# Row statistics of the attention read at the head of a chunk, and those of the first output tiles later

## The chip, the core and the metric

The kernel runs on one core of a Trainium2 chip. Its time is device time in microseconds (us). The engines are named as in the profile: PE is TensorE (matrix products; PEld its weight loads), DVE is VectorE, ACT is ScalarE, POOL is GpSimd, SP issues most of the DMAs. Each engine takes its instructions strictly in its own order and waits at an instruction until what it needs has been signalled by the others.

## What is computed

One layer of a streaming encoder for 1024 prompt frames, 64 frames of a running stream and 16 meta tokens, width 1024. One input projection gives queries, keys, values, gates and the inputs of a convolution. One half is attention over chunks of 64 frames (own chunk, two before it, the meta tokens, a learned sink per head), the other a causal depthwise convolution of width 31 with LayerNorm, SiLU and a pointwise product. Both halves are RMS-normalised per frame, multiplied by a SiLU gate, and go through one output projection:

```python
y = concat([rms(att, g_att) * silu(ga), rms(conv, g_conv) * silu(gb)]) @ w_out
h = h + rms(y, g_post)
```

The two inner `rms` need, per frame, one over the root of a mean of squares over 512 channels. These are the row statistics of the title: `ra` for the attention half, `rc` for the convolution half.

## The kernel before, in words

The frames lie in three column groups (0 to 384, 384 to 768, 768 to 1104). Input products are units `g` of 24 matmuls each (weight tile and frames split in a high and a low part, three products): `g19_1` is weight tile 19, column group 1. A unit's result lies in one PSUM bank until its reader has taken it: for the attention gate tiles (12 to 15) and the last convolution gate tile (19) the reader is ACT (a tanh) and then DVE (`ga` or `gb`, a multiplication that is put off by some steps). Three banks with the tag `mm` serve these units, the `ra` and the `var` alike (`mm_ps`, line 125). A bank is given to the next tile that asks for one when its last reader so far is known; the bank whose reader was recorded first goes first.

The units wait in a queue. The attention loop (lines 959 to 1007) goes through the 17 chunks in the order 16 (the running stream), 0, 1, ... 15, and puts `fill(n)`, that is n matmuls of the queue, between its own steps, so that PE has work while the other engines do theirs. In turn i it records: the score products `s` of chunk order[i] with four DVE passes that read them (`att_scores`, line 651), gate multiplications, the products `av` with the values for chunk order[i-2] (`att_values`, 719), the split `qs` of the next queries (`att_prep`, 646), the transposes `pa` and `pb` for chunk order[i-1] (`att_transpose`, 703), the exponentials, the normalisation `T` (`norm`, 679), and, at the end of the turn, `att_stats` for chunk order[i-3]. From turn L0 on (that of chunk 11) LayerNorm steps stand among them, for three column groups n: `ln_pre` sums four channel tiles on DVE, `ln_mean` is a product `mu`, a subtraction on DVE, squares on ACT (`vq`) and their sums on POOL, `ln_var` is three tiny products `var` and their DVE reads `rln`, `ln_diag` prepares a diagonal on DVE (`sqc`), `ln_scale` is a product `rstd` and a multiplication of `H` on DVE.

`att_values` also leaves, for each tile of two chunks, the sum of squares over channels in `asq` (ACT squares, two POOL additions). `att_stats` (740) turns it into row statistics: a product `ra` of `asq` with a column of ones into a bank `mm`, a DVE operation `ra4t` (for tile 4) that reads it, and a power on POOL.

The last stage is the pointwise product `pw` (four column groups by four tiles) with a small task of a list, `plan`, behind each of the 16: the letters l, h are the splits of the output weights, M, n the splits of an output tile's operands (ACT, DVE), and `r0`, `r1` are `rc_rstd(0)` and `rc_rstd(1)` (line 1081): a product `rc` into the one bank `av`, a DVE operation `rc0t`, a power on POOL. Then come the output tiles T = 0, 1, 8, 2, ... 7, each with products `y`; `rc_rstd(T + 1)` is called behind the last product of tile T where it hasn't been called yet, and `rc_rstd(0)` and `rc_rstd(8)` within tile 0.

The order of each engine's instructions is that in which they are recorded; only two counters, which estimate how far PE, DVE and ACT have got (`given`, line 67), decide on which of ACT and DVE a few operations go, and put off others.

Of the kernel before, what the change touches and what calls it, by code (L numbers as in the profile page):

```python
# [33 lines left out]
NCHUNK = SEQ // HD  # L34
# [14 lines left out]
def layer_kernel(ctx: ExitStack, tc: tile.TileContext, x, x_fm, w_in, w_pw, w_out, vec, g_post,  # L49
# [70 lines left out]
    def chunks(ap):  # L120
        return ap.rearrange("p (c q) -> p c q", q=HD)
# [3 lines left out]
    def mm_ps(name):  # L125
        banks[0] += 1
        run_due(lambda p: p[1] and p[1] <= banks[0] - 3)
        return ps_tile("mm", 3, name)
# [61 lines left out]
    def hi_w(p, on_dve=False, dst=None, a=0, b=KT):  # L190
        m = WORDER[p]
        load_raw(p)
        if not a:
            pre[m] = dst or (wp.tile([P, KT, P], F32R, tag="whi", name=f"whi{m}"),
                             wp.tile([P, KT, P], F32R, tag="wlo", name=f"wlo{m}"))
        raw, hi = halves[a] if p == 2 else raws[p][:, a:b], pre[m][0][:, a:b]
        if on_dve:
            dve.tensor_copy(hi, raw)
        else:
            act.activation(hi, raw, AF.Copy)  # L200

    def lo_w(p, a=0, b=KT, on_dve=False):
        hi, lo = (t[:, a:b] for t in pre[WORDER[p]])
        raw = halves[a] if p == 2 else raws[p][:, a:b]
        if p > 3 and not on_dve and freer() == "act":
            act.activation(lo, hi.bitcast(F32), AF.Copy, scale=-1.0)
            pool.dma_start(out=lo, in_=raw, accum_op=ALU.add)
            return
        dve.tensor_tensor(out=lo, in0=raw, in1=hi.bitcast(F32), op=ALU.subtract)
# [189 lines left out]
    def fill(k):  # L399
        for _ in range(min(k, len(queue))):  # L400
            queue.pop(0)()
            tick()
# [189 lines left out]
    def row_rstd(src, r, dst, name, ps):  # L592
        for o in range(0, P, r):
            mm(ps[o:o + r, 0:2], lhsT=src, rhs=ones_m[:, 0:2], start=True, stop=True)
        r = P
        t = sm.tile([P, 1], F32, tag="rr", bufs=2, name=name + "t")
        dve.tensor_scalar(out=t[:r], in0=ps[:r, 0:1], scalar1=RMS_EPS, scalar2=None,
                                op0=ALU.add)
        pool.tensor_tensor(out=dst[:r], in0=t[:r], in1=mhalf[:r], op=ALU.pow)
# [46 lines left out]
    def att_prep(c):  # L646
        qs = kqs[c] = sm.tile([P, 2, 4, HD], F32R, tag="qs", bufs=2, name=f"qs{c}")
        act.activation(qs[:, 0], qb[:, c], AF.Copy)
        dve.tensor_tensor(out=qs[:, 1], in0=qb[:, c], in1=qs[:, 0].bitcast(F32), op=ALU.subtract)
# [41 lines left out]
    def att_v(c):  # L691

        if c % 2 == 0:
            nc.sync.dma_start(vE[MB:MB + HD], vtok[:HD, c // 2])
            avs[c] = [(NKEY, vE)]
            if c:
                avs[c].insert(0, (2 * HD, vcache if c == NCHUNK else vtok[:, c // 2 - 1]))
        else:
            if c > 1:
                nc.sync.dma_start(vO[:HD], vtok[HD:, c // 2 - 1])  # L700
            avs[c] = [(HD + MB, vO if c > 1 else vE), (NKEY, vtok[:, c // 2])]

    def att_transpose(c):
        lo, T = att[c]
        pt = slot("P", f"PT{c}", (P, 2, 512))
        att[c] = []
        for n, (end, v) in enumerate(avs.pop(c)):
            k = end - lo
            ps = ps_tile("pt", 2, f"p{'ab'[n]}{c}")
            for i in range(4):  # L710
                tp(ps[:k, i * P:(i + 1) * P], T[:, i, lo:end], ident)
            if freer() == "act":
                act.activation(pt[:k, n, :], ps[:k, :], AF.Copy)
            else:
                dve.tensor_copy(pt[:k, n, :], ps[:k, :])
            att[c].append((k, v, pt[:, n]))
            lo = end

    def att_values(c):
        sample = c == NCHUNK  # L720
        av = ps_tile("av", 1, f"av{c}")
        last = len(att[c]) - 1
        for n, (k, v, pt) in enumerate(att[c]):
            for g in range(2):
                mm(av[g * HD:(g + 1) * HD, :256], lhsT=v[:k, g * HD:(g + 1) * HD],
                   rhs=pt[:k, g * 256:(g + 1) * 256], start=n == 0, stop=n == last)
        av4 = av[:, :256].rearrange("p (t q) -> p t q", t=4)
        act.activation(qb[:, c], av4, AF.Copy)
        Tt = c // 2
        if Tt not in asq:  # L730
            asq[Tt] = sm.tile([P, 4, P], F32, tag="asq", bufs=2, name=f"asq{Tt}")
        o = (c % 2) * HD
        act.activation(asq[Tt][:, :, o:o + HD], qb[:, c], AF.Square)
        if c % 2 or sample:
            w = HD if sample else P
            s = asq[Tt]
            pool.tensor_tensor(out=s[:, 0:2, :w], in0=s[:, 0:2, :w], in1=s[:, 2:4, :w], op=ALU.add)
            pool.tensor_tensor(out=s[:, 0, :w], in0=s[:, 0, :w], in1=s[:, 1, :w], op=ALU.add)

    def att_stats(Tt):  # L740
        w = HD if Tt == 8 else P
        row_rstd(asq[Tt][:, 0, :w], w, ra[:, Tt:Tt + 1], f"ra{Tt}", mm_ps(f"ra{Tt}"))
# [11 lines left out]
    h1, h2 = (0, 4), (4, KT)  # L754
# [127 lines left out]
    def gate_att(ready, most=12):  # L882
        for g in [g for g in gas if all(c in ready for c in range(g[2] // HD, g[3] // HD))][:most]:
            gas.remove(g)
            t, n, c0, c1, gt = g
            dst = qb[:, c0 // HD:c1 // HD, t, :]
            dve.tensor_tensor(out=dst, in0=dst, in1=chunks(gt[:, :c1 - c0]), op=ALU.mult)
# [64 lines left out]
    order = [NCHUNK] + list(range(NCHUNK))  # L952
# [5 lines left out]
    i = -1  # L958
    while (i := i + 1) < max(len(order) + 2, L0 + 7 if L0 < 99 else 0):
        left = len(order) + 1 - i  # L960
        if L0 == 99 and i >= 9 and (i == 12 or len(taps) < 2):
            L0 = i
        quota = (max(24, -(-(len(queue) - REST) // left)) if i else 48) if left > 0 else 26
        n = i - L0
        if i < len(order):
            exps, norm = att_scores(order[i])
        if n > 0:
            gate_att(order[:max(0, i - 2)], 2)
        if 2 < i <= len(order) + 1:
            att_values(order[i - 2])  # L970
        if 1 < i < len(order):
            att_v(order[i])
        if i == len(order) + 1:
            hi_w(len(WORDER) - 1, on_dve=True, dst=[sm.tile([P, KT, P], F32R, tag=t, bufs=1, name=f"w1{t}")
                                          for t in ("kT", "vT")])
            lo_w(len(WORDER) - 1, on_dve=True)
        if i + 1 < len(order):
            att_prep(order[i + 1])
        fill((32 if i == 1 else 4) if left > 0 else 0)
        if 0 < i <= len(order):  # L980
            att_transpose(order[i - 1])
        if i < len(order):
            exps()
        fill(8 if left > 0 else 4)
        if n == 0:
            while taps:
                f, j = taps.pop(0)
                f(j)
            sqc = sm.tile([P, HW], F32, tag="sq", bufs=1, name="sqc")
        for step, at in ((ln_pre, (0,1,3)), (ln_diag, (2, 4, 6))):  # L990
            if n in at:
                step(at.index(n))
        if i < len(order):
            norm()
        fill(8 if left > 0 else 4)
        if i == 1:
            att_values(order[0])
            att_v(order[1])
        if 3 <= i < len(order) + 3:
            c = order[i - 3]  # L1000
            if c % 2 or c == NCHUNK:
                att_stats(c // 2)
        for step, d in ((ln_mean, 0), (ln_var, 1), (ln_scale, 2)):
            if n - d in (0, 2, 4):
                fill(2)
                step((n - d) // 2)
        fill((quota - 20 if left > 0 else 8) - (2 if 0 <= n <= 6 else 0))
# [99 lines left out]
    drain()  # L1107
    run_due(lambda p: True)

    plan = "G0,l1,h2 l2,h3 l3,S2 h4 z2 l4,h5 l5,S3 h6 z3,h7 l6,M0 l7,r0 n0 . r1 M1 n1".split()  # L1110
    for n in range(4):
        for m in range(4):
            pointwise(n, m, [pre[PW], pre[PW + 1]])
# [136 lines left out]
```

## Time and profile before

| | before |
|---|---|
| time, median of 3 runs | 483.17 us (482.18 to 485.7) |
| the profiled execution | 482.85 us |
| its span (first to last instruction) | 481.1 us |
| busy: PE, DVE, ACT, POOL | 461.8, 380.0, 231.9, 75.0 us |
| mean granted clock of PE in the span | 0.986 |

The span leaves out 1.75 us of the profiled execution that lie around it. A clock of 1 stands for the higher of PE's two levels, 2.4 GHz; 0.5 is the lower, 1.2 GHz.

### The profile page before, as it was taken

What the parts mean: (1) busy time and instruction counts of PE and PEld (TensorE: products, weight loads), DVE (VectorE), ACT (ScalarE), POOL (GpSimd) and SP (SyncE); (2) the same over time, 40 slices, a digit from 0 to 9 for tenths busy, and PEclk for the clock granted to TensorE, in tenths of its full rate; (3) what the DMA queues carried; (4) which work ended last, traced back from release to release, by engine and by line L of the source; (5) the groups of instructions that cost most, each with busy time, mean ns of one, the idle gap of its engine ahead of it and who ended that gap; (6) DMA issues with size and microseconds to landing.
All of it is one profiled execution on the core that took longest, in us unless ns stands there. A gap on an engine that the chain in (4) does not pass through costs nothing.

```text
span 481.1 us, 7432 instructions
## 1 busy us (share of the span) xinstructions
PE 461.8 (96%) x2809; PEld 420.3 (87%) x2809; DVE 380.0 (79%) x671; ACT 231.9 (48%) x535; POOL 75.0 (16%) x106
## 2 busy tenths in 40 slices
PE   8999999999999999999999996989998999999994
PEld 7999999999999999988889885868898887888884
DVE  3669999999999999988999995666999545645443
ACT  6675432135133225567667755545787325433322
POOL 0000100003010000001201223232224501111100
PEclk9999999999999999999999998889999999999998
DMA  8992244044033334230110101011243212222231
GB/s 275 402 330 97 44 102 114 0 110 131 4 82 89 90 88 93 67 92 4 51 35 19 50 4 47 5 48 44 89 132 131 89 65 89 65 89 88 87 122 54
DMA packets 16491, 43.54 MB, mean 91 GB/s; under 512 B 2600, under 2 KB 4888, under 8 KB 16456
## 3 DMA queue, kind: packets, MB, share of 16 engines
q1 hardware_dynamic: 14584, 37.31, 22.9%
q0 software_dynamic: 1872, 5.77, 6.4%
q8 instruction: 22, 0.36, 0.3%
q14 instruction: 13, 0.11, 0.1%
HBM read 32.00 MB, written 4.84 MB: 77 GB/s over the span
## 4 chain that ended last, share of the span: by engine, by line
PE 75%; DVE 11%; ACT 2%; issue 1%; DMA 1%; POOL 0%; DVEq 0%; POOLq 0%; ACTq 0%
PE g L104 44%; PE y L104 20%; PE av L104 3%; PE s L104 3%; DVE H L86 2%; DVE wo L86 2%; PE pa L108 1%; DVE sqc L86 1%; PE pb L108 1%; DMA woraw<-in_w_out_dram 1%; DVE qb L86 1%; DVE T L86 1%; ACT T L86 1%; PE pw L104 1%; DVE zl L86 1%
## 5 line engine op out<-in xcount | busy, mean ns | idle before, releaser
L104 PE MATMUL g<-xT,whi 128*128 128x384 f32 (+2 forms) x960 | 225.4, 334 | 0.4 <-DVE xT L86 0.2
L104 PEld LDWEIGHTS g<-xT,whi 128*128 128x128 f32 x960 | 169.0, 189 | 8.9 <-issue 6.1
L86 DVE SCALAR_TENSOR_TENSOR H<-u,vec_t,H 128x1118 f32<-128x1118 f32 x120 | 166.5, 1388 | 3.2
L104 PE MATMUL g<-xT,wlo 128*128 128x384 f32 (+2 forms) x480 | 139.6, 333 | 0.5 <-DVE wlo L86 0.5
L104 PEld LDWEIGHTS g<-xT,wlo 128*128 128x128 f32 x480 | 88.3, 189 | 2.7 <-issue 1.2
L104 PE MATMUL y<-wo,mh 128*128 128x512 f32 (+2 forms) x304 | 89.0, 381 | 0.0
L104 PEld LDWEIGHTS y<-wo,mh 128*128 128x128 f32 (+1 forms) x304 | 55.2, 185 | 11.5
L104 PE MATMUL y<-wo,ml 128*128 128x512 f32 (+1 forms) x136 | 51.2, 378 | 0.0
L86 DVE SCALAR_TENSOR_TENSOR y<-y,small,y 128x512 f32<-128x512 f32 (+1 forms) x19 | 13.7, 721 | 32.8 <-PE y L104 29.4
L86 ACT ACTIVATE T<-T,st 128x210 f32<-128x210 f32 (+2 forms) x85 | 37.0, 450 | 5.0 <-DVE st L86 4.9
L86 POOL DMA_DIRECT2D wlo<-wraw x13 | 11.5, 885 | 148.8 <-ACT wlo L86 123.7
L104 PEld LDWEIGHTS y<-wo,ml 128*128 128x128 f32 x136 | 25.6, 188 | 4.5
L86 ACT ACTIVATE yj<-y 128x512 f32<-128x512 f32 (+2 forms) x21 | 12.8, 608 | 31.7 <-DVE y L86 31.6
L104 PE MATMUL g<-xT,wq 128*128 128x384 f32 (+1 forms) x144 | 25.4, 333 | 0.0
L86 ACT ACTIVATE whi<-wraw 128x1024 fp32r<-128x1024 f32 (+1 forms) x23 | 22.4, 978 | 6.1 <-PE g L104 6.1
L104 PEld LDWEIGHTS g<-xT,wq 128*128 128x128 f32 x144 | 24.2, 188 | 0.5
L86 DVE CUSTOM_DVE_ANT_0 T<-s,bias 128x210 f32<-128x210 f32 (+2 forms) x68 | 20.6, 359 | 3.9 <-PE s L104 3.7
L86 ACT ACTIVATE sg<-g 128x384 f32<-128x384 f32 (+1 forms) x10 | 4.7, 474 | 36.5 <-PE g L104 36.5
L86 ACT ACTIVATE y<-y,small 128x512 f32<-128x512 f32 (+1 forms) x19 | 12.6, 665 | 18.5 <-PE y L104 18.4
L86 ACT ACTIVATE qb<-av 128x256 f32<-128x256 f32 x17 | 6.4, 379 | 30.6 <-PE av L104 30.6
L86 ACT ACTIVATE qb<-g 128x384 f32<-128x384 f32 (+1 forms) x12 | 5.7, 474 | 32.1 <-PE g L104 32.1
L86 DVE TENSOR_TENSOR y<-y,gpost 128x512 f32<-128x512 f32 (+2 forms) x19 | 12.5, 659 | 6.5 <-ACT yj L86 6.3
(199 smaller groups left out, 617.2 us busy)
## 6 DMA issues: line engine op xcount, KB each, us to landing
wraw<-in_w_in_dram SPq DMA_DIRECT2D x18, 512.0 KB, 3.4
wlo<-wraw POOLq DMA_DIRECT2D x9, 512.0 KB, 4.6
H<-in_x_dram SPq DMA_DIRECT2D x8, 512.0 KB, 8.4
xr<-in_x_dram SPq DMA_DIRECT2D x8, 512.0 KB, 3.9
out_dram<-o SPq DMA_DIRECT2D x7, 512.0 KB, 2.9
woraw<-in_w_out_dram SPq DMA_DIRECT2D x5, 512.0 KB, 3.4
wraw<-in_w_in_dram SPq DMA_DIRECT2D x8, 256.0 KB, 5.9
x<-in_x_fm_dram SPq DMA_DIRECT2D x4, 384.0 KB, 6.2
```

What stands on the lines that cost most here:

```text
L86: ins = op(*a, **k)
L104: return tc.keep_in_program_order(nc.tensor.matmul(out, lhsT=lhsT, rhs=rhs, **k))
L108: return tc.keep_in_program_order(nc.tensor.transpose(*a, **k))
```

## The change

`att_stats` is called at another place of the same turn, ahead of `att_values`, and two entries of `plan` move: `r0` by two tasks, and `r1` is gone from the list, so that `rc_rstd(1)` is called by the output tile 0.

```diff
         if n > 0:
             gate_att(order[:max(0, i - 2)], 2)
+        if 3 <= i < len(order) + 3:
+            c = order[i - 3]
+            if c % 2 or c == NCHUNK:
+                att_stats(c // 2)
         if 2 < i <= len(order) + 1:
             att_values(order[i - 2])
...
         if i == 1:
             att_values(order[0])
             att_v(order[1])
-        if 3 <= i < len(order) + 3:
-            c = order[i - 3]
-            if c % 2 or c == NCHUNK:
-                att_stats(c // 2)
         for step, d in ((ln_mean, 0), (ln_var, 1), (ln_scale, 2)):
...
-    plan = "G0,l1,h2 l2,h3 l3,S2 h4 z2 l4,h5 l5,S3 h6 z3,h7 l6,M0 l7,r0 n0 . r1 M1 n1".split()
+    plan = "G0,l1,h2 l2,h3 l3,S2 h4 z2 l4,h5 l5,S3 h6 z3,h7 l6,M0 l7 n0 r0 . M1 n1".split()
```

How this moves instructions is seen at three places. The first is PE in the turn of chunk 12, the first in which a LayerNorm step `var` stands. Before, `ra4` and `var0` stand two rows apart, in the unit g19_2:

```order
L104 MATMUL g19_2_2984<-xT2_92,wlo19_2613 128x320
L104 MATMUL ra4_3002<-ones_m_78,asq4_2751 128x2
L104 MATMUL g19_2_2984<-xT2_92,whi19_2612 128x320 x2
L104 MATMUL var0_3010<-ones_m_78,sqc_2885 128x2 x3
L104 MATMUL g19_2_2984<-xT2_92,wlo19_2613 128x320
```

With the change `ra4` stands at the head of the turn, between the chunk's scores and the products with the values:

```order
L104 MATMUL s12_0_2920<-ky_1086,qs12_2846 128x210
L104 MATMUL s12_1_2921<-ky_1086,qs12_2846 128x210
L104 MATMUL ra4_2942<-ones_m_78,asq4_2756 128x2
L104 MATMUL av10_2947<-PT10_2853,vtok_88 64x256 x2
L104 MATMUL av10_2947<-PT10_2853,vE_86 64x256 x2
```

So `ra4` went ahead by 18 rows of PE, to another place of the same turn, and `var0` kept its own. The same holds for ra5 and var1 two turns later and for ra6 and var2.

The second place is DVE in the same turn, from the gate multiplications to the reads of `var0`. Before:

```order
L86 TENSOR_TENSOR qb_627<-qb_627,ga1_0_2609 128x6x64
L86 TENSOR_TENSOR qs13_2951<-qb_627,qs13_2951 128x256
L86 TENSOR_TENSOR wlo14_2882<-wraw14_2526,whi14_2881 128x1024
L86 TENSOR_TENSOR sqc_2885<-H_89 128x384
L86 TENSOR_TENSOR sqc_2885<-sqc_2885,H_89 128x384 x2
L86 RECIPROCAL st12_2935<-st12_2935 128x4
L86 TENSOR_SCALAR T12_2934<-T12_2934,st12_2935 128x210
L86 TENSOR_SCALAR ra4t_3004<-ra4_3002 128x1
L86 SCALAR_TENSOR_TENSOR gb3_2877<-gb3_2877,g19_1_2880 128x384
L86 MEMSET rln0_3011 128x4
L86 TENSOR_SCALAR rln0_3011<-var0_3010 128x1 x3
```

And with the change:

```order
L86 TENSOR_TENSOR qb_627<-qb_627,ga1_0_2614 128x6x64
L86 TENSOR_SCALAR ra4t_2944<-ra4_2942 128x1
L86 TENSOR_TENSOR qs13_2956<-qb_627,qs13_2956 128x256
L86 TENSOR_TENSOR wlo14_2882<-wraw14_2526,whi14_2881 128x1024
L86 TENSOR_TENSOR sqc_2885<-H_89 128x384
L86 TENSOR_TENSOR sqc_2885<-sqc_2885,H_89 128x384 x2
L86 RECIPROCAL st12_2935<-st12_2935 128x4
L86 TENSOR_SCALAR T12_2934<-T12_2934,st12_2935 128x210
L86 SCALAR_TENSOR_TENSOR gb3_2877<-gb3_2877,g19_1_2880 128x384
L86 MEMSET rln0_3011 128x4
L86 TENSOR_SCALAR rln0_3011<-var0_3010 128x1 x3
```

`ra4t`, the read of `ra4`, went ahead of the split of the queries, of a weight split and of the sums; the rest keeps its order.

The third place is PE in the pointwise products. Before, `rc0` and `rc1` stand ten rows apart:

```order
L104 MATMUL rc0_3766<-ones_m_78,sqc_2885 128x2
L104 MATMUL pw2_3_3771<-zh2_3638,w1kT_3413 128x280 x4
L104 MATMUL pw2_3_3771<-zh2_3638,w1vT_3414 128x280 x4
L104 MATMUL pw2_3_3771<-zl2_3639,w1kT_3413 128x280 x4
L104 MATMUL pw3_0_3790<-zh3_3720,whi22_3431 128x278 x4
L104 MATMUL pw3_0_3790<-zh3_3720,wlo22_3432 128x278 x4
L104 MATMUL pw3_0_3790<-zl3_3721,whi22_3431 128x278 x4
L104 MATMUL pw3_1_3805<-zh3_3720,whi22_3431 128x278 x4
L104 MATMUL pw3_1_3805<-zh3_3720,wlo22_3432 128x278 x4
L104 MATMUL pw3_1_3805<-zl3_3721,whi22_3431 128x278 x4
L104 MATMUL rc1_3822<-ones_m_78,sqc_2885 128x2
```

With the change `rc0` stands six rows later, and no `rc` is among the rest of the pointwise products:

```order
L104 MATMUL pw3_0_3785<-zl3_3721,whi22_3430 128x278 x4
L104 MATMUL rc0_3800<-ones_m_78,sqc_2885 128x2
L104 MATMUL pw3_1_3805<-zh3_3720,whi22_3430 128x278 x4
L104 MATMUL pw3_1_3805<-zh3_3720,wlo22_3431 128x278 x4
L104 MATMUL pw3_1_3805<-zl3_3721,whi22_3430 128x278 x4
L104 MATMUL pw3_2_3822<-zh3_3720,w1kT_3413 128x278 x4
```

`rc1` now stands behind the last product of output tile 0, `y0_1_0`, and ahead of the first of tile 1.

## Rows read from the trace of the kernel before

**Rows 1.** The page: PE's busy time, and its granted clock in 40 slices.

```profile
PE 461.8 (96%) x2809; PEld 420.3 (87%) x2809; DVE 380.0 (79%) x671; ACT 231.9 (48%) x535; POOL 75.0 (16%) x106
...
PEclk9999999999999999999999998889999999999998
```

**Rows 2.** Waits of PE: who waits for whom, total us, times, longest us.

```profile
PE var L104 <- DVE ra4t L86: 4.1, 1, 4.1
PE var L104 <- DVE ra5t L86: 2.3, 1, 2.3
PE rc L104 <- DVE rc0t L86: 1.5, 1, 1.5
```

**Rows 3.** Timeline of PE around var0: start us, us, instruction, [idle before, releaser].

```profile
285.48 0.92 PE L104 MATMUL s<-ky,qs 64*128 64x210 f32 x12
...
286.32 0.65 PE L104 MATMUL av<-PT,vtok 128*64 128x256 f32 x4
...
291.56 0.28 PE L104 MATMUL ra<-ones_m,asq 128*128 128x2 f32 x2
291.70 0.54 PE L104 MATMUL g<-xT,whi 128*128 128x320 f32 x2
296.30 0.80 PE L104 MATMUL var<-ones_m,sqc 128*128 128x2 f32 x6 [4.05 <-DVE ra4t L86]
...
302.36 1.05 PE L108 MATMUL pa<-ident,T 128*128 128x128 f32 x4
```

**Rows 4.** Timeline of DVE, around ra4t and at two gate multiplications.

```profile
292.42 0.42 DVE L86 TENSOR_TENSOR qs<-qb,qs 128x256 fp32r<-128x256 f32 x1 [2.49 <-ACT qs L86]
...
295.76 0.33 DVE L86 TENSOR_SCALAR T<-T,st 128x210 f32<-128x210 f32 x1
296.00 0.15 DVE L86 TENSOR_SCALAR ra4t<-ra 128x1 f32<-128x1 f32 x1
296.07 0.54 DVE L86 SCALAR_TENSOR_TENSOR gb<-gb,g 128x384 f32<-128x384 f32 x1
...
313.01 2.10 DVE L86 TENSOR_TENSOR qb<-qb,ga 128x384 f32<-128x384 f32 x2
...
321.70 0.55 DVE L86 TENSOR_TENSOR qb<-qb,ga 128x384 f32<-128x384 f32 x1
```

**Rows 5.** Timeline of ACT: the last normalisation pieces of chunk 12.

```profile
295.76 1.19 ACT L86 ACTIVATE T<-T,st 128x210 f32<-128x210 f32 x3 [0.22 <-DVE st L86]
```

**Rows 6.** Timeline of POOL: sums of squares ahead of ra4, var0 and var1.

```profile
280.62 1.33 POOL L86 TENSOR_TENSOR asq<-asq 128x256 f32<-128x256 f32 x2 [1.74 <-ACT asq L86]
...
291.44 1.01 POOL L86 TENSOR_TENSOR sqc<-sqc,vq 128x384 f32<-128x384 f32 x1 [0.63 <-ACT vq L86]
...
311.30 3.39 POOL L86 TENSOR_TENSOR sqc<-sqc,vq 128x384 f32<-128x384 f32 x3 [7.82 <-ACT vq L86]
```

**Rows 7.** Windows: us, busy of PE, PEld, DVE, ACT, POOL, granted clock, DMA.

```profile
296.30:300.00 3.70, 3.70 (x24) 2.94 (x26) 1.28 (x10) 0.65 (x2) 1.34 (x2) 0.60 0.14 52
300.00:304.00 4.00, 4.00 (x19) 2.97 (x16) 1.35 (x7) 1.65 (x5) 1.24 (x2) 0.51 0.03 8
...
318.30:322.00 3.70, 3.63 (x29) 2.41 (x30) 2.17 (x14) 0.06 (x1) 1.40 (x2) 0.86 0.11 24
322.00:326.00 4.00, 4.00 (x20) 3.87 (x21) 1.37 (x3) 2.37 (x8) 1.19 (x2) 0.70 0.17 55
...
370.00:380.00 10.00, 8.48 (x57) 7.79 (x56) 8.73 (x17) 4.80 (x11) 7.12 (x8) 1.00 0.32 102
```

**Rows 8.** Timeline of PE around the transposes of chunk 13 and var1.

```profile
311.69 0.60 PE L108 MATMUL pa<-ident,T 128*82 128x128 f32 x4
312.13 0.60 PE L108 MATMUL pb<-ident,T 128*128 128x128 f32 x4
...
315.75 0.34 PE L104 MATMUL g<-xT,whi 128*128 128x384 f32 x1
318.37 0.80 PE L104 MATMUL var<-ones_m,sqc 128*128 128x2 f32 x6 [2.28 <-DVE ra5t L86]
```

## The prediction

> **What bounds the kernel now.** I read the page first: TensorE is busy 461.8 of 481.1 us, and its granted clock falls below full only in three neighbouring slices and at the very end [rows 1]. So the time is TensorE's work plus its few stalls. Next, TensorE's own waits: apart from the start, three are over a microsecond, 4.1, 2.3 and 1.5 us [rows 2]. All three have one form: a small matmul that prepares a row statistic (var, rc) waits for VectorE to have read the result of another small statistic (ra4t, ra5t, rc0t). The timeline of TensorE shows the first place: ra4 runs at 291.56, two matmuls of a g unit follow, and var0 starts only at 296.30 [rows 3]. VectorE shows why: ra4t, an operation of 0.15 us, stands behind qs, a weight split, three sums and the first normalisation T, and is reached at 296.00 [rows 4]. var0 starts 0.15 us after ra4t ends (296.15) and before the gate multiplication behind it ends (296.61), so it is ra4t's bank that it waits for. The windows give the second price: after each of the two long stalls TensorE works at the lower of its two levels (1.2 instead of 2.4 GHz) for a while; the mean clock is 0.60 and 0.51 in the two windows after the first, 0.86 and 0.70 after the second [rows 7].
>
> **What moves, and what each piece costs.** No instruction is added or removed. Moved are ten small groups: eight times ra (one or two tiny matmuls, one VectorE operation of 0.15 us [rows 4], one POOL power), and rc0 and rc1 of the last stage. They issue no DMA; on SP only gpost and the second xr load swap places, two loads of the output stage. On POOL the powers of ra keep their places behind the sums; rc0's goes behind one more sum and rc1's to the output stage. Since the recording counters run a little differently, three gate multiplications stand a few rows later on VectorE, and one normalisation piece of chunk 15 goes from ScalarE to VectorE, 0.33 us [rows 4]; both lie in stretches that term 7 covers.
>
> Term 1, var0. ra4's matmul now stands right behind the scores s12, and ra4t behind the two gate multiplications, ahead of qs. There VectorE sat idle for 2.49 us until qs was released at 292.42 [rows 4], so ra4t costs nothing; without that cover it would cost its 0.15 us. ra4's input, the POOL sum asq, is there at 280.62 + 1.33 = 281.95 [rows 6], 4.4 us before the end of the scores (285.48 + 0.85 = 286.33) [rows 3]; so it waits for nothing. var0 then waits for its other input alone, the last POOL sum of squares, done at 291.44 + 1.01 = 292.45 [rows 6]. TensorE has been free since 291.70 + 0.54 = 292.24 [rows 3]. New start 292.50, instead of 296.30: **-3.80**.
>
> Term 2, the clock after it. In the windows 296.30 to 300 and 300 to 304 the clock lost 3.70 x 0.40 + 4.00 x 0.49 = 3.44 us [rows 7]. With a stall of a quarter of a microsecond I take it that the clock stays up: **-3.44**.
>
> Term 3, what is late next. The transposes pa of chunk 12 begin 6.06 us behind var0 (302.36) [rows 3], of which the clock took 1.48 + 2.36 x 0.49 = 2.64; at full clock they would begin at 292.50 + 3.42 = 295.92. Their fourth quarter needs the last normalised T, which ScalarE ends at 295.76 + 1.19 = 296.95 [rows 5]; that chain starts from qs at 292.42 and is not moved. One transpose takes (312.13 - 311.69)/4 = 0.11 us [rows 8], so the fourth would start at 296.25 and must wait until 297.00: **+0.75**.
>
> Term 4, var1. The same at ra5: the stall of 2.28 us in front of 318.37 [rows 8]. Its POOL sums end at 311.30 + 3.39 = 314.69 [rows 6], before TensorE is through with its work at 315.75 + 0.34 = 316.09 [rows 8], so nothing of the stall is left: **-2.28**. Term 5, the clock after it: 3.70 x 0.14 + 4.00 x 0.30 = 1.72 [rows 7]: **-1.72**.
>
> Term 6, rc1. It no longer stands in the pointwise loop but behind the first output tile, as the later tiles' rc already do, and rc0 now has nothing waiting behind it: the 1.51 us go [rows 2], **-1.51**. rc1's own matmul costs the same there, and the reader of its result, the eviction of the next output tile, comes twelve matmuls later.
>
> Term 7, unknown: TensorE now runs into VectorE's chain earlier. VectorE's idle times behind var0 are used up, and H times rstd must be through before the transposes pb can take its bank. For chunk 13 I follow VectorE from 296.0 with the durations of before: gate and statistic reads to 296.8, four score passes to 298.0, qs, copy and diagonals to 299.6, the wait for ScalarE's four exponentials to 300.4, normalisation to 301.5, mean, gate, H times rstd to 305.4. TensorE reaches pb at 312.13 - 6.49 = 305.64 [rows 8]. A margin of 0.2 us is none. For chunk 15 the like wait exists already. I bound the two together between 0 and 2.0 us (a pair of multiplications beside POOL's sums took 2.10 us where one without them took 0.55 [rows 4], so such an overlap can stretch a chain by 1.0) and take the middle: **+1.0**.
>
> The stretch of VectorE beside POOL is what the Trainium skill describes (page "SBUF — State Buffer", section "SBUF: two separate sides"): an operation of VectorE with two SBUF inputs and a POOL operation that reads SBUF exclude each other for the whole instruction. The 2.10 against 0.55 us agree. The H operations on TensorE's path read PSUM and one SBUF tile, so by that rule they would not be held up, and the sum would lose term 7 and come out at 471.2, inside the forecast's own spread.
>
> Sum: -3.80 - 3.44 + 0.75 - 2.28 - 1.72 - 1.51 + 1.0 = -11.0. The profiled execution's span of 481.1 becomes 470.1, and with the 1.75 us around the span (482.85 - 481.1) 471.9. The median of the runs before, 483.17, lies 0.3 above that execution; so **472.2 us**.
>
> **Rivals.** (a) The stalls go, but the clock still falls once. Left near 292 to 297 are a stall of 0.26 and one of 0.75 us. For it: the two falls of before follow directly on idle time. Against it: behind the wait of 1.51 us the clock stayed at 1.00 [rows 7], and what is left is shorter. It gives back 3.44: 475.6 us. (b) VectorE becomes the bound at more places than term 7's two, at the score passes of chunk 15 and at its normalisation too: two further waits of 1.0 us, 474.2 us. For it speaks the margin of 0.2; against it, that VectorE still had idle stretches such as the 2.49 us ahead of qs [rows 4]. (c) The change does not do what it says: var0 waits for another bank, that of the unit g19_1, whose gate multiplication still stands where it stood (296.07 to 296.61). Then both long stalls stay and only term 6 is won: 481.7 us. Against it: the waits named by the built program count VectorE up to ra4t for var0 and to ra5t for var1, in both kernels. (d) Slower: the head of a chunk is a bad place for ra, since TensorE works in order and everything of the chunk stands behind it. If POOL's sums came late, each of the eight ra would stall it. The point from which that costs is 4.4 us of lateness [rows 3, 6]; if POOL were 6.7 us later, eight stalls of 2.3 us with the clock lost behind each (1.7 us, term 5) cost 32 us and leave 504 us. Against it: POOL's longest sums here take 3.39 us in a row [rows 6], and POOL is busy 16% of the span [rows 1].
>
> **Numbers.** The forecast 60%, (a) 15%, (b) 11%, (c) 9%, (d) 5%. Low end: no term 7, no wait at pa (0.75), and the half microsecond that runs scatter: 469.9. High end: (a) with another 1.0 us of (b): 476.6. Together that holds the forecast, (a) and (b). A measurement of this kernel can tell a change of about 1% from none: 478.3 and below is faster, so faster 86%, same 9%, slower 5%.
>
> **What would show it.** var0 starts within half a microsecond of the third POOL sum, and var1 without a wait; the granted clock falls in no slice but the last; rc1's wait is gone from TensorE's list; the transposes pa of chunk 12 wait under a microsecond for T; ra waits nowhere. Wrong I am if a clock below 1.00 stands anywhere in 285 to 320, if pb waits over a microsecond, or if var still waits for VectorE.

## The result, and the profile after

| | before | with the change |
|---|---|---|
| median of the runs, side by side on one chip | 484.44 us (482.18 to 485.75, 4 runs) | 470.84 us (470.50 to 471.21, 4 runs) |
| ratio, with 95% interval | | 0.9724 [0.9679, 0.9769] |
| the profiled execution, its span | 482.85, 481.1 us | 470.69, 468.9 us |
| mean granted clock of PE in the span | 0.986 | 0.997 |

The change makes the kernel 2.8% faster; a second measurement, listed with the experiments, gave 0.9735 [0.9702, 0.9768]. The page of the changed kernel, PE's line and the granted clock in 40 slices, answers to [rows 1]:

```profile
PE 456.2 (97%) x2809; PEld 416.7 (89%) x2809; DVE 380.1 (81%) x672; ACT 231.3 (49%) x534; POOL 75.0 (16%) x106
...
PEclk9999999999999999999999999999999999999998
```

PE is busy 5.6 us less with the same 2809 matmuls: the three slices of low clock are gone, and only the last one is left. PE's waits, total us, times, longest us, answer to [rows 2]:

```profile
PE warm_ps L104 <- POOL rx L86: 1.4, 1, 1.4
PE pw L104 <- DVE zl L86: 1.0, 2, 0.5
...
PE rstd L104 <- DVE sqc L86: 0.7, 1, 0.7
...
PE pb L108 <- DVE H L86: 0.4, 1, 0.4
...
PE pw L104 <- DVE zh L86: 0.2, 1, 0.2
PE var L104 <- POOL sqc L86: 0.2, 1, 0.2
```

The three long waits (4.1, 2.3 and 1.5 us) are not in the list. What var still waits for is its own input. The timeline of PE (start, us, instruction, idle before and releaser) answers to [rows 3] and [rows 8]:

```profile
284.56 0.92 PE L104 MATMUL s<-ky,qs 64*128 64x210 f32 x12
...
291.59 0.83 PE L104 MATMUL var<-ones_m,sqc 128*128 128x2 f32 x6 [0.18 <-POOL sqc L86]
295.39 1.05 PE L108 MATMUL pa<-ident,T 128*128 128x128 f32 x4
...
302.60 0.38 PE L104 MATMUL ra<-ones_m,asq 128*128 128x2 f32 x2
304.74 0.60 PE L108 MATMUL pa<-ident,T 128*82 128x128 f32 x4
305.17 0.60 PE L108 MATMUL pb<-ident,T 128*128 128x128 f32 x4
308.76 0.72 PE L104 MATMUL var<-ones_m,sqc 128*128 128x2 f32 x6
...
320.94 0.66 PE L108 MATMUL pb<-ident,T 128*128 128x128 f32 x4 [0.41 <-DVE H L86]
```

The scores s12 (first row) begin 0.92 us earlier than before (284.56 against 285.48). That lead is 0.94 us already at the first scores (188.35 us before), ahead of anything that was moved, and is no work of the change: the scores s12 lie between 0.8 us later and 1.7 us earlier from one experiment's profile to the next. (mu, var and rstd are numbered by column group: mu1 stands ahead of var1, rstd1 behind it.) All that follows is counted from it. var0 leads by 296.30 - 291.59 = 4.71, var1 by 318.37 - 308.76 = 9.61.

DVE around ra4t answers to [rows 4]:

```profile
288.94 0.14 DVE L86 TENSOR_SCALAR ra4t<-ra 128x1 f32<-128x1 f32 x1
291.51 0.45 DVE L86 TENSOR_TENSOR qs<-qb,qs 128x256 fp32r<-128x256 f32 x1 [2.42 <-ACT qs L86]
...
294.87 0.33 DVE L86 TENSOR_SCALAR T<-T,st 128x210 f32<-128x210 f32 x1
295.12 0.55 DVE L86 SCALAR_TENSOR_TENSOR gb<-gb,g 128x384 f32<-128x384 f32 x1
```

ra4t now stands in front of DVE's idle time of 2.42 us, which was 2.49, and so costs nothing. The sums on POOL, and the pieces T on ACT, answer to [rows 6] and [rows 5]:

```profile
279.70 1.33 POOL L86 TENSOR_TENSOR asq<-asq 128x256 f32<-128x256 f32 x2 [6.99 <-ACT asq L86]
...
290.52 1.01 POOL L86 TENSOR_TENSOR sqc<-sqc,vq 128x384 f32<-128x384 f32 x1 [0.64 <-ACT vq L86]
```

```profile
294.87 1.19 ACT L86 ACTIVATE T<-T,st 128x210 f32<-128x210 f32 x3 [0.25 <-DVE st L86]
```

The sum for ra4 ends at 281.03, 4.4 us ahead of its matmul, which stands right behind the scores, at 285.40; the third sum of squares at 291.53, and var0 starts 0.06 us later. The windows over the same work as [rows 7] (us, busy of PE, PEld, DVE, ACT, POOL, granted clock, DMA):

```profile
291.59:295.29 3.70, 3.70 (x32) 2.79 (x32) 3.60 (x8) 3.45 (x13) 0.45 (x1) 1.00 0.29 66
295.29:299.29 4.00, 3.97 (x26) 3.52 (x25) 3.78 (x18) 3.97 (x16) 2.08 (x3) 1.00 0.21 78
308.76:312.46 3.70, 3.70 (x33) 2.81 (x33) 3.51 (x19) 1.39 (x3) 0.86 (x1) 1.00 0.12 39
312.46:316.46 4.00, 4.00 (x29) 3.90 (x28) 3.41 (x10) 3.05 (x12) 2.99 (x2) 1.00 0.14 44
...
355.00:365.00 10.00, 9.40 (x72) 8.86 (x70) 9.54 (x14) 6.27 (x13) 4.56 (x5) 1.00 0.27 94
```

The clock is 1.00 where it was 0.60, 0.51, 0.86 and 0.70. The last row shows what TensorE comes up against next: in the pointwise loop DVE is busy 9.54 of 10 us, PE 9.40.

### The profile page after: what moved, and what is told of

Same layout as the page of the kernel before. It is cut to its first block, busy times and chain, and to the rows that moved or that the text cites. A ratio compares the mean times of both kernels' runs of the same rounds, so it can differ in the third digit from the quotient of the medians.

```text
span 468.9 us, 7427 instructions
## 1 busy us (share of the span) xinstructions
PE 456.2 (97%) x2809; PEld 416.7 (89%) x2809; DVE 380.1 (81%) x672; ACT 231.3 (49%) x534; POOL 75.0 (16%) x106
## 4 chain that ended last, share of the span: by engine, by line
PE 85%; DVE 8%; DMA 2%; ACT 2%; issue 1%; POOL 1%; SPq 0%; DVEq 0%; POOLq 0%; ACTq 0%
PE g L104 53%; PE y L104 20%; PE av L104 3%; PE s L104 3%; DVE wo L86 2%; DVE H L86 2%; PE pa L108 2%; PE pb L108 1%; DMA x<-in_x_fm_dram 1%; DMA woraw<-in_w_out_dram 1%; DVE wlo L86 1%; POOL sqc L86 1%; DVE qb L86 1%; DVE zl L86 1%; DVE sqc L86 0%
## 5 line engine op out<-in xcount | busy, mean ns | idle before, releaser
L104 PE MATMUL g<-xT,whi 128*128 128x384 f32 (+2 forms) x960 | 222.8, 332 | 1.1 <-ACT xT L86 0.9
L86 POOL TENSOR_TENSOR asq<-asq 128x128 f32<-128x128 f32 (+2 forms) x18 | 12.7, 707 | 38.5 <-ACT asq L86 37.8
```

What stands on the lines that cost most here:

```text
L86: ins = op(*a, **k)
L104: return tc.keep_in_program_order(nc.tensor.matmul(out, lhsT=lhsT, rhs=rhs, **k))
```

## The experiments

"Lead" below is the start of a matmul in the profile of before minus its start in that of the run, less the lead that the run already has at s12; it is worked out from the two traces. Ratios are to the kernel before, measured beside each run (its medians were 483.4 to 484.9 us).

### The two parts of the change apart

```diff
 # e1: the kernel after, with the plan of before
-    plan = "... l6,M0 l7 n0 r0 . M1 n1".split()
+    plan = "... l6,M0 l7,r0 n0 . r1 M1 n1".split()
 # e2: the kernel before, with the plan of after
-    plan = "... l6,M0 l7,r0 n0 . r1 M1 n1".split()
+    plan = "... l6,M0 l7 n0 r0 . M1 n1".split()
```

> The row statistics ra at the head of the chunk, as in the change; rc0 and rc1 stay in the pointwise loop, as before. Theory (the stalls of var0 and var1 and the clock behind them make up the gain, the tile statistics rc only their 1.5 us): var0 and var1 wait for no DVE statistic, no granted clock under 1.0 between 285 and 325 us, the wait rc <- rc0t of 1.5 us is back; time 0.7 to 1.5 us above the changed kernel, a ratio to the kernel before of 0.974 to 0.976. Rival (the new place of rc0 and rc1 carries much of the gain): 0.985 or more.

> Only rc0 and rc1 in their new places; the row statistics ra stay at the end of the chunk. Theory: both long stalls of var (4.1 and 2.3 us) and the low clock behind each stay, only the wait of 1.5 us of rc1 goes, of which the pointwise loop and the first output tile give some back: 0.7 to 1.5 us less than before, a ratio of 0.997 to 0.9985. Rival (the plan carries the gain): 0.985 or less.

ra alone: 471.96 us, 0.9747 [0.9722, 0.9772], as expected. The plan alone: 482.05 us, 0.9953 [0.9925, 0.9981]. The move of ra carries 12.5 of the 13.6 us; the plan adds 1.1 to it (471.96 - 470.84). Alone the plan gave more than was expected, 2.3 us by the ratio, but its interval reaches down to 0.9, and its executions spread from 479.8 to 484.2 us, since both stalls and the low clock are still in them. The lead of the run with ra alone is that of the change to within 0.1 us up to the pointwise loop, where the wait of rc1, which it still has, leaves it 1.1 us short.

### The bank, not the place

```diff
 # e3: ra unmoved, its product in the bank av; e8: in a bank pt
-        row_rstd(..., f"ra{Tt}", mm_ps(f"ra{Tt}"))
+        row_rstd(..., f"ra{Tt}", ps_tile("av", 1, f"ra{Tt}"))    # e3
+        row_rstd(..., f"ra{Tt}", ps_tile("pt", 2, f"ra{Tt}"))    # e8
```

> The kernel before with one thing changed: the product of the row statistics ra stands in the PSUM bank of the tag av instead of one of the three of the tag mm, so that var no longer gets its bank. ra stays at the end of the chunk in program order, on TensorE and on VectorE. Theory (the wait for the bank, not the place): var0 and var1 start without a wait for a statistic, the clock stays at 1.0 there; 9 to 11 us less than before, a ratio of 0.977 to 0.982, if the next av does not wait in its turn. Rival 1 (the place in the chunk makes the gain): within 1 us of before, 0.998 to 1.002. Rival 2 (the wait moves to av, which now needs the reading of ra): the stall appears in front of av of the next chunk, with 2 to 4 us and the clock behind it; 0.985 to 1.0.

> The kernel before with one thing changed: the product of the row statistics ra stands in one of the two PSUM banks of the tag pt, whose next user is the transposes pb of the chunk after, instead of one of the three of the tag mm. ra stays at the end of the chunk on TensorE and on VectorE. Theory (it is the bank and who takes it next, not the place): var0 and var1 wait for no statistic, pb does not wait for ra4t (which is read at 296, some 3 us ahead of it), the clock stays up: a ratio of 0.974 to 0.977, as with ra moved and rc not. Rival 1 (the bank's next user always pays, as av did with 1.7 us and the clock behind): pb waits over 1 us and the time stays at 0.982 or more. Rival 2 (the place): 0.998 to 1.002.

Neither edit changes the bank alone: `mm_ps` also counts its calls and lets postponed gate multiplications go by that count, so with ra out of it some of them stand a few rows later on DVE. They do not explain var0: it starts ahead of the next of them in both runs, 4.0 us with av and 2.8 us with pt.

With av: 476.05 us, 0.9837 [0.9810, 0.9863], between theory and rival 2. The timeline of PE in this run:

```profile
293.09 0.83 PE L104 MATMUL var<-ones_m,sqc 128*128 128x2 f32 x6
...
296.85 0.65 PE L104 MATMUL av<-PT,vO 82*64 82x256 f32 x4 [1.68 <-ACT T L86]
```

var0 waits for nothing, but the next av does, for 1.68 us. The row names ACT's T; what av reads of ACT, and what read its bank last, show which it is:

```profile
293.37 0.58 ACT L86 ACTIVATE PT<-pb 128x512 f32<-128x512 f32 x1
```

```profile
296.60 0.15 DVE L86 TENSOR_SCALAR ra4t<-ra 128x1 f32<-128x1 f32 x1
```

PT was there at 293.95; ra4t ended at 296.75, 0.10 us ahead of av. An earlier av waits too, for 0.67 us at 251.15, where before it had no wait: ra1t had ended 0.10 us ahead of it as well, the piece T that the row names 0.50 ahead. So the wait went over to the bank's next user, and the releaser that the row names is the wrong one. Behind it the clock was 0.5 from 297.5 to 300.9. At ra5, where DVE is less late (ra5t ends 0.17 us ahead of av), av does not wait, and that part of the gain is whole.

With pt: 474.24 us, 0.9784 [0.9742, 0.9826]. In its profiled execution (471.69 us, the lowest of four) var0 and var1 wait for nothing, pb does not wait for ra4t, the clock stays at 1.00, and the lead at the end is 9.5 us, against 10.1 with ra moved alone: nearly all of the gain with ra where it was. A part came back at another place, since ra4 itself now has to wait until ACT has taken the transposes that stood in its bank:

```profile
291.36 0.35 PE L104 MATMUL ra<-ones_m,asq 128*128 128x2 f32 x2 [1.29 <-ACT PT L86]
...
291.95 0.72 PE L104 MATMUL var<-ones_m,sqc 128*128 128x2 f32 x6
```

The other three executions took 474.1 to 476.1 us at clocks of 0.990 to 0.993 instead of 0.996, so in them the clock fell somewhere; no trace shows where. That the place of ra earns no more than some half a microsecond by itself is shown for the profiled execution; the 2.3 us by which the median misses the run with ra moved are not explained: the wait of 1.3 us and the lower clock in three executions are candidates.

### The clock

```diff
 # e4: the kernel before; in ln_var(n), ahead of var
+        for _ in range((16, 9, 0)[n]):
+            nc.tensor.matmul(av_of_this_turn[:, 256:256 + P], lhsT=ident, rhs=ident, start=True, stop=True)
```

> The kernel before with 16 and 9 matmuls of the identity put on TensorE ahead of var0 and var1; their products go to unused columns and nothing reads them. At 0.23 us each (the start of the program has 11 of them in 5.06 us at half clock) they fill 3.7 of the 4.05 us and 2.1 of the 2.28 us; var still waits for the reading of ra4 and ra5 and starts when it did. Theory (the clock falls because of the idle time): the granted clock stays at 1.0 in 285 to 325 us, and 3.4 + 1.7 = 5.1 us are won, less up to 1 us where TensorE then meets VectorE: a ratio of 0.989 to 0.992. Rival (the clock falls for another reason there, so the idle time is the whole price): the clock falls as before, ratio 1.000 to 1.003.

479.25 us, 0.9901 [0.9866, 0.9937]. PE in this run:

```profile
292.34 0.28 PE L104 MATMUL ra<-ones_m,asq 128*128 128x2 f32 x2
...
292.85 3.73 PE L532 MATMUL av<-ident 128*128 128x128 f32 x32
297.08 0.80 PE L104 MATMUL var<-ones_m,sqc 128*128 128x2 f32 x6 [0.49 <-DVE ra4t L86]
...
313.79 2.17 PE L532 MATMUL av<-ident 128*128 128x128 f32 x18
316.34 0.80 PE L104 MATMUL var<-ones_m,sqc 128*128 128x2 f32 x6 [0.38 <-DVE ra5t L86]
...
370.16 0.38 PE L104 MATMUL rc<-ones_m,sqc 128*128 128x2 f32 x2 [1.53 <-DVE rc0t L86]
```

var0 starts as late as ever (its lead is 0.0), yet 50 added matmuls make the kernel faster. From var0 to mu1 the lead grows by 3.1 us and from var1 to mu2 by 1.6, where 3.44 and 1.72 were expected. With the stalls filled the clock stayed up, so the low clock follows from the idle time and is a price of its own; DVE's order is that of the kernel before, row for row. All four executions ran at 0.994 to 0.997, where none of the kernel before was above 0.988. The run also has a new low stretch, behind the wait of rc1, which cost 1.6 us:

```profile
371.50:374.90 3.40, 3.40 (x17) 3.40 (x16) 1.55 (x5) 2.25 (x5) 2.77 (x5) 0.50 0.40 149
285.00:371.50 86.50, 82.21 (x585) 73.49 (x585) 71.70 (x155) 56.00 (x128) 27.77 (x30) 1.00 0.22 69
```

### Two of the eight

```diff
 # e5 and e6: the kernel before; at the head of the turn
+                if c // 2 == 4:        # e6: == 5
+                    att_stats(c // 2)
 # and at its old place
+                if c // 2 != 4:        # e6: != 5
                     att_stats(c // 2)
```

> The kernel before, with ra4 alone of the nine row statistics at the head of its chunk; the plan as before. Theory (each late ra costs by the bank that it hands on, and by nothing else): var0 starts without its wait and the clock stays up behind it; var1 still waits for ra5t, for 2.0 to 3.0 us, with the low clock behind; 6 to 7 us less than before, a ratio of 0.985 to 0.988. Rival (moving all of them matters, or what is won at var0 is lost at var1): 0.993 or more.

> The kernel before, with ra5 alone at the head of its chunk; the plan as before. Theory: the wait of 4.1 us at var0 and its low clock stay, the wait of 2.3 us at var1 goes with the 1.7 us of clock behind it: 3.5 to 4.5 us less than before, a ratio of 0.990 to 0.993; together with the run that moves ra4 alone it makes up what moving all nine gave (0.975), so that the seven others are worth nothing. Rival: the seven others carry part of it, so that the two together fall short of moving all by over 2 us.

The two texts count nine moved statistics; eight are moved, as the prediction has it. ra7 is called once behind the loop in both kernels.

ra4 alone: 473.97 us, 0.9794 [0.9753, 0.9835], more than expected. ra5 alone: 479.32 us, 0.9892 [0.9858, 0.9927], a little more. PE with ra4 alone:

```profile
292.11 0.83 PE L104 MATMUL var<-ones_m,sqc 128*128 128x2 f32 x6 [0.18 <-POOL sqc L86]
...
311.20 0.80 PE L104 MATMUL var<-ones_m,sqc 128*128 128x2 f32 x6 [1.86 <-DVE ra5t L86]
```

The two gains come to 3.1% (each interval is some 0.4% wide to either side) where all eight gave 2.5%. The clock scatters in these times: the profile of ra4 alone, 476.93 us, is the slowest of four executions, and the other three ran at a higher clock. The leads tell it more sharply: with ra4 alone 6.34 us are won from s12 to mu1 (the terms 1 to 3 summed to 6.49), with ra5 alone 4.01 from mu1 to mu2, 10.35 together; with all eight moved (e1) it is 10.36 from s12 to mu2. So the six others are worth nothing there.

### Three tries at the pointwise loop

```diff
-    plan = "G0,l1,h2 l2,h3 l3,S2 h4 z2 l4,h5 l5,S3 h6 z3,h7 l6,M0 l7 n0 r0 . M1 n1".split()
+    plan = "G0,l1,h2 l2,S2 h3 z2,l3 h4 l4,S3 h5 z3,l5 h6 l6,M0 h7,l7 n0 r0 . M1 n1".split()     # e7
+    plan = "G0,l1,h2,S2 l2,h3 l3,z2 S3 h4 l4,h5 l5,z3 h6 l6,h7 M0 l7 n0 r0 . M1 n1".split()     # e9
+    plan = "G0,l1,h2,S2 l2,h3 z2 l3,h4 . l4,h5 l5,S3 h6 z3,h7 l6,M0 n0 l7 r0 . M1 n1".split()   # e11
 # e9 as well, in split_z
-        dve.tensor_copy(zh[:, :, :w], hc)
+        (act.activation(zh[:, :, :w], hc, AF.Copy) if n > 1 else dve.tensor_copy(zh[:, :, :w], hc))
```

> The changed kernel with another plan of the pointwise loop: S2, z2, S3 and z3 one task or two earlier, the weight pieces l3, l5, h3 to h7 behind them; rc0 at the same place. What it aims at is what the changed kernel still waits for in that loop: zh 0.19 and zl 0.52 and 0.51 us. Theory (these waits are VectorE's splits standing behind weight pieces): they go, 1.0 to 1.2 us less than the changed kernel, 469.6 to 469.9 us, a ratio to the kernel before of 0.969 to 0.971. Rival (the weight pieces pushed back, or the products H that VectorE now reads later, make TensorE wait in their turn): 0.972 or more.

> The changed kernel with the casts zh2 and zh3 of the pointwise loop on ScalarE instead of VectorE (0.73 us each there), S2 put in ScalarE's idle stretch at 341 us and S3, z2 and z3 one to three tasks earlier; the weight pieces keep their order. It aims at the 0.19, 0.52 and 0.51 us that TensorE still waits for zh and zl there, and at the 0.4 us for ml in front of the first output tile. Theory (that stretch is bound by VectorE, and a shift of places alone gave the time back at ml, so VectorE must be given less to do): these waits go, 1.0 to 1.6 us less than the changed kernel in the same session, ratio to it 0.9966 to 0.998. Rival (ScalarE's casts come later than VectorE's did, or the products H that VectorE reads later hold TensorE's banks): no gain or up to 2 us lost.

> The changed kernel with three tasks of the pointwise loop at other places and nothing on another engine: S2 behind h2, so that the split z2 can stand ahead of the weight piece l3 (2.1 us on VectorE), and n0 (the split ml of the first output tile) ahead of the weight piece l7 (1.27 us), which the first output tile reads last. Theory, after the two runs that lost at ml and at ScalarE's casts: VectorE works without a pause from 332 to 365 us, so an earlier z2 alone would only make the wait for ml longer, and n0 ahead of l7 takes that wait away: the 0.19 and one 0.52 us at z and the 0.4 us at ml go, 0.6 to 1.1 us less than the changed kernel (470.6), ratio to the kernel before 0.971 to 0.973. Rival: l7 then comes late for the end of the first output tile, or the products H wait behind z2 and l3; no gain, or some 1 us lost.

e7: 474.98 us, 0.9817 [0.9782, 0.9852]. e9: 472.81, 0.9772 [0.9737, 0.9808]. e11: 470.71, 0.9737 [0.9704, 0.9769]. None beats the change, which gave 470.56 beside e9; each time the rival came true. e7 and e9 show why in one line each, the wait of the first output product that reads ml. In the change it cost 0.4 us of lead:

```profile
367.39 0.50 PE L104 MATMUL y<-wo,ml 128*128 128x512 f32 x1 [3.04 <-DVE ml L86]
```

```profile
367.06 0.50 PE L104 MATMUL y<-wo,ml 128*128 128x512 f32 x1 [1.10 <-DVE ml L86]
```

DVE works almost without pause through this loop, so what is put ahead of something is given back at the loop's end; and where a weight piece on ACT came later, DVE had to wait for it (3.13 us in e9). e11 did lose the wait for zh at z2, one of the two for zl and the one at ml, and got a longer one at z3. Behind it and a wait of 0.52 us the clock fell, in the profiled execution, the slowest of six (472.34 us):

```profile
357.42 0.78 PE L104 MATMUL pw<-zh,whi 128*128 128x278 f32 x4 [1.12 <-DVE zh L86]
```

```profile
359.50:362.90 3.40, 3.40 (x17) 3.40 (x17) 3.40 (x7) 1.84 (x4) 1.30 (x2) 0.50 0.00 0
```

### The change again

> The changed kernel again, beside the run with zh on ScalarE and the kernel before. Theory (the clock behind a stall costs more or less from one execution to the next, so that a kernel with no stall over a microsecond in it repeats closely while the kernel before spreads): all executions within 1 us of 470.8, the granted clock of each 0.995 or more, while those of the kernel before range over 4 us and 0.974 to 0.986. Rival (spread is a matter of the session): the changed kernel spreads over 3 us too.

470.56 us (470.24 to 472.13), 0.9735 [0.9702, 0.9768]; clocks of 0.995 to 0.998. Five of the six executions lie within 0.6 us of the 470.8 expected, one is 1.3 away. The kernel before ranged from 480.26 to 486.19 us beside it, at clocks of 0.977 to 0.988. So here the spread goes with the stalls, and the one execution apart ran at a clock of 0.997, so its 1.6 us lie elsewhere. A stall does not always bring spread, though: the four executions with ra5 alone, which still have the stall of 4.05 us, lie within 0.3 us.

## Why the prediction was right, step by step

The forecast was 472.2 us within 469.9 to 476.6; it is 470.84. By leads:

| step | predicted | measured |
|---|---|---|
| 1, var0's wait | -3.80 | -3.79 (lead 0.92 to 4.71) |
| 2 and 3, clock behind it, wait of pa for T | -3.44 + 0.75 = -2.69 | -2.56 (4.71 to 7.27, at mu1) |
| 4, var1's wait | -2.28 | -2.34 (7.27 to 9.61) |
| 5, clock behind it | -1.72 | -1.85 (9.61 to 11.46, at the second matmul of rstd1) |
| 6, rc1 | -1.51 | -1.1 (the change against ra alone) |
| 7, DVE met earlier | +1.0 (0 to 2.0) | +0.5, and not where it was put |
| sum | -11.0 | -11.2 (0.92 to 12.09) |

**Terms 1 to 5.** Terms 1, 4 and 5 hold, each within 0.15 us. Terms 2 and 3 hold only as a sum. pa of chunk 12 did wait for T: its four transposes took 1.05 us where those of pb behind them took 0.60, so 0.45 of the 0.75 that the step gave for it. With that, the clock gave back 2.56 + 0.45 = 3.01 us and not 3.44. The step took it that work at the low clock takes twice as long, and from var0 to pa it put 3.42 us at full clock; it is 3.80. The scores s show it: from their start to that of the first product av, 1.54 us before (at 0.5) and 0.85 with the change (at 1.00), 1.8 times and not twice:

```profile
297.69 1.61 PE L104 MATMUL s<-ky,qs 64*128 64x210 f32 x12
299.23 1.12 PE L104 MATMUL av<-PT,vO 82*64 82x256 f32 x4
```

```profile
292.75 0.92 PE L104 MATMUL s<-ky,qs 64*128 64x210 f32 x12
293.60 0.65 PE L104 MATMUL av<-PT,vO 82*64 82x256 f32 x4
```

**Term 6** was too large by 0.4: the matmul of rc1 no longer waits, but TensorE comes to the first output tile sooner than VectorE's split ml, and its lead falls there from 12.76 to 12.36. The step took for granted that nothing was late next.

**Term 7** was mis-sized at both places that it named. For chunk 13 the walk along VectorE was good: H times rstd was to end at 305.4 and ends at 304.47, which with the start's 0.92 is 305.39:

```profile
302.72 1.75 DVE L86 TENSOR_TENSOR H<-H,rstd 128x1536 f32<-128x1536 f32 x1
```

But pb comes at 305.17, which is 306.09 by the same count, and not at 305.64: ra5's own matmuls (the row at 302.60 in the timeline above, 0.3 us) now stand ahead of it. This step had left them out; the rest is what terms 2 and 3 fell short by. So the margin was 0.7 and not 0.2. For chunk 15 the wait is 0.41, as before (0.39). Instead 0.45 us are lost in the pointwise loop, at the first products with zh of column group 2 (the wait of 0.19 us is new; the one for zl behind it, 0.52, was 0.53 before), with and without the new plan: the lead there falls from 11.42 to 10.97 with the change and from 11.33 to 10.88 with ra alone. The rule of the Trainium skill (page "SBUF — State Buffer", section "SBUF: two separate sides") that would have taken term 7 away is borne out at its place: H times rstd took 1.75 us with POOL sums of 3.61 us begun beside it at 303.39, and H minus mu, at 300.59 with none beside it, took 1.75 as well.

**From the sum to the median.** That the sum comes so near is in part luck: term 6 was 0.4 too large and term 7 charged 0.5 too much, and in terms 2 and 3 errors of 0.43 and 0.30 stand against each other. The forecast lies 1.4 us above the median: 0.9 are the earlier start, 0.2 the sum, 0.1 is won behind the last product, and of the 0.3 added for the step from the profiled execution to the median only 0.15 came (470.84 - 470.69). The ratio came out lower still (472.2 to 483.17 would be 0.977) because the kernel before is slower than its profile: beside all the runs its executions ran from 480.26 us at a mean clock of 0.988 to 486.19 at 0.974, with medians of 483.4 to 484.9, and the profiled one, at 0.986, had paid less for its stalls than most. The 5.16 us of terms 2 and 5 are thus a low price of the clock: in the profile of the plan alone (484.23 us) PE works 9.04 and 10.15 us in its two low stretches, which at half speed would be 9.6 us lost, an estimate and by terms 2 and 3 rather too high.

**Rivals.** (a) The clock does not fall again: behind s12 the longest wait left is 0.74 us. (b) VectorE did not become the bound where it was feared, but holds TensorE up in the pointwise loop, for half a microsecond, and again at ml. (c) var0 waited for ra4t's bank: with the change it starts at 291.59, and the gate multiplication that the rival names is only at 295.12; e5, which moves ra4 alone, has the same. (d) ra waits nowhere at the head of the chunk.

## What to carry to other kernels

A statistic's tiny matmul can hold up TensorE if its PSUM bank was last read by an operation that is queued late on another engine; read such a result early, or give the bank to something whose next user is far off, and look who the next user is, since the wait moves to it. Price a stall of TensorE with the low clock behind it, and take that price from several executions. Where the engine beside it is busy nearly all the time, as VectorE is here in the pointwise loop, reordering its work only moved the wait.

## What was not expected of the hardware

The low stretch behind one and the same stall is not the same from run to run. Behind a wait of 4.05 us for ra4t it lasted 6.8 us in the profile of before and 10.2 us in two others; behind 2.28 us it lasted 3.4, behind 1.95 us 10.2. The two long ones of the run with the plan alone (the first began 1.2 us ahead of var0, while TensorE was still waiting):

```profile
294.57:304.80 10.23, 9.04 (x43) 7.28 (x44) 4.13 (x19) 3.92 (x12) 2.66 (x4) 0.50 0.16 53
318.46:328.69 10.23, 10.15 (x45) 8.25 (x46) 3.56 (x16) 2.78 (x10) 2.59 (x4) 0.50 0.09 30
```

Nor does the length of a wait decide alone whether the clock falls. Behind the 1.5 us at rc1 it stayed up in the profile of before and fell in e4, and it fell behind 1.12 and 0.52 us, 1.8 us apart, in e11. Behind 3.04 us ahead of the output tile, in e7, it stayed at 1.00 with TensorE busy for 0.96 of 4 us:

```profile
364.00:368.00 4.00, 0.96 (x5) 0.55 (x5) 3.51 (x7) 1.13 (x3) 1.57 (x3) 1.00 0.39 131
368.00:372.00 4.00, 4.00 (x19) 3.33 (x18) 2.77 (x6) 2.91 (x7) 3.17 (x4) 1.00 0.36 135
```

What decides it these runs leave open. The forecast's argument against its rival (a), that the clock stayed up behind 1.51 us and what is left is shorter, was therefore weaker than it looked, though behind the 0.74 us and less that the change leaves it did not fall in its two profiles.
